# A two-layer DiT block on one core: fewer context columns in three projections, and scheduling priority for norm steps and evacuations

## The chip, the cores and the metric

The kernel runs on one core of a Trainium2 chip. A core has TensorE (matrix products, stationary operand loaded by a weight load, result in PSUM), VectorE, ScalarE and GpSimd, which run beside each other and wait for each other through semaphores, and DMA queues; all large loads here are issued by SyncE. The metric is the device time of one execution in microseconds, as a median over runs.

## The reference

Two layers work on 256 context rows and 256 latent rows of width 1024. Only the latent rows are returned, so in the last layer the context rows are needed for keys, values and recurrent states alone (`with_ctx` is false there).

```python
for l in range(DEPTH):                       # DEPTH = 2
    with_ctx = l < DEPTH - 1
    hx = rmsnorm(x, g_pre_mix[l]) * (1.0 + ax1) + sx1      # ax1, sx1, gx1 ...: c @ w_ada
    hc = rmsnorm(ctx, g_pre_mix[l]) * (1.0 + ac1) + sc1
    pc, px = split_cols(hc @ w_in + b_in), split_cols(hx @ w_in + b_in)
    # three mixers: mLSTM (q k v o i f), HGRN2 (q f i g), differential attention (q k v)
    yx = jnp.concatenate([mx, gx, ax], axis=-1) @ w_out    # and yc if with_ctx
    x = x + gx1 * rmsnorm(yx, g_post_mix[l])
    hx = rmsnorm(x, g_pre_ffn[l]) * (1.0 + ax2) + sx2
    x = x + gx2 * rmsnorm(swiglu(hx, ...), g_post_ffn[l])
    # the same for ctx if with_ctx
```

## The kernel before

**Rows and tiles.** The 512 rows are four tiles of 128: tiles 0 and 1 are context, 2 and 3 latent. `halves` is (1, 0) in the first layer (`full` is true there) and (1,) in the second: half 1 are tiles 2 and 3, half 0 tiles 0 and 1. `qt` is the list of tiles with queries: all four in the first layer, 2 and 3 in the second.

**Split products.** Each product is made of three matmuls on rounded f32 (fp32r). An operand is split into an upper part and the rest. Activations lie transposed in `hT[0]` and `hT[1]`. Weights come in blocks of 512 KB by SyncE (`wraw`, 3 buffers), ScalarE rounds them to `whi` (L297), VectorE subtracts to `wlo` (L298), with 2 buffers each and a priority of AHEAD = 2000. `mm` (L302) issues every one of these matmuls; the stationary operand is always 128 by 128.

**Projections.** `gemm_tm(srcs, act, tiles, evac, pre)` (L324) puts row tiles on the PSUM partitions: the activations are stationary and 256 weight columns move, for each of the tiles and 8 blocks of k. Two tiles share one PSUM bank, and an evacuation (`add_bias` L912, `ev_vo` L1062) takes a bank at a time. The differential attention's query, key columns (`O_DAQ`, 768 wide) go in three products of 256 columns, i = 0, 1, 2; so do the mLSTM's value and output gate (`O_MLV`) and query and key (`O_MLQ`). In each of these three groups the product i = 1 straddles the border at column 384 between two of the parts. `gemm_cm` (L368) keeps weights stationary and moves 256 or 512 activation columns; the feed-forward's gate and up projections use it.

**Between attention and feed-forward.** `head_norm` (L649) normalizes a head's output and writes it to Y; `rstd` (L412) does the power on GpSimd (L415, L416). `y_T` (L1147) transposes Y on TensorE and evacuates it with the gains into `hT` (ScalarE L1157, VectorE L1158). `out_first` and `out_rest` multiply with `w_out` (k blocks 4 to 7 first). `ev_z` (L1172) multiplies the result with the gate row on VectorE (L1175) and sums its squares on ScalarE (L1177). `post_norm` (L468) finishes that norm (VectorE L471, GpSimd L473) and adds the residual (VectorE L475). `norm_rows` (L424) squares R on ScalarE (L426), takes the power on GpSimd and scales on VectorE (L428). `norm_T` (L436) transposes that on TensorE (L447 ahead, L455) and evacuates it with scale and shift (ScalarE L461, VectorE L463), rounds to `hT[0]` (ScalarE L465) and subtracts to `hT[1]` (VectorE L466). `norm_T` also serves the next layer's first norm.

**Modulation.** The vectors for later stages are made from `w_ada` by VectorE sums (L226, L228: `acc`, `accq` from `araw`, 2 buffers) which the generator `ada_group` yields one by one; `ada_step` takes one after each weight block, and `ada_flush` the rest.

**Order.** The order on each engine is written out at compile time by a scheduler, which takes from the ready instructions of an engine the one of best priority; priority is the place in the program text, and `with tc.high_priority(offset=N)` moves instructions N places ahead. CHAIN is 4000. On the chip each engine then follows its written order and waits at its head. In the first layer the steps after attention have no such block; in the second one they have in part:

```python
if full:
    for t in (2 * hf, 2 * hf + 1):
        post_norm(t, Z[t], zss[t])
    norm_T(u1, s1_, hf, scr, ahead=False)
else:
    with tc.high_priority(offset=CHAIN):
        norm_T(u1, s1_, hf, scr)
```

Of the kernel before, what the change touches and what calls it, by code (L numbers as in the profile page):

```python
# [101 lines left out]
def dit_block(ctx: ExitStack, tc: tile.TileContext, x, c, ctx_in, c_ctx, w_ada, b_ada, g_pre_mix,  # L102
# [201 lines left out]
    def upper(ps, blk, act, t, first):  # L304
        hi, _, ks = blk
        for kk, k in enumerate(ks):
            mm(ps, act(0, k, t), hi[:, kk], first and kk == 0, False)
            mm(ps, act(1, k, t), hi[:, kk], False, False)

    def lower(ps, blk, act, t, last):  # L310
        _, lo, ks = blk
        for kk, k in enumerate(ks):
            mm(ps, act(0, k, t), lo[:, kk], False, last and k == ks[-1])

    def blocks_of(srcs, holds=None):

        k0 = 0
        for si, pieces in enumerate(srcs):
            nk, n = pieces[0].shape[0] // P, sum(p.shape[-1] for p in pieces)
            hi, lo = wload(pieces, holds and holds[si])  # L320
            yield hi[:, :, :n], lo[:, :, :n], range(k0, k0 + nk)
            k0 += nk

    def gemm_tm(srcs, act, tiles, evac, pre=None):  # L324

        n = sum(p.shape[-1] for p in srcs[0])
        tiles = list(tiles)
        wide = n > 256  # L330
        bank = lambda t: t if wide else t // 2
        banks = {b: pst([P, 512] if wide else [P, 2, 256], mm=True) for b in sorted({bank(t) for t in tiles})}
        dst = lambda t: banks[t][:, :n] if wide else banks[bank(t)][:, t % 2, :n]
        new = lambda t: wide or t - 1 not in tiles or t % 2 == 0
        for si, blk in enumerate(blocks_of(srcs)):
            end = si == len(srcs) - 1
            if pre is not None and end:
                pre()
            if wide and end:
                for t in tiles:  # L340
                    upper(dst(t), blk, act, t, si == 0)
                    lower(dst(t), blk, act, t, True)
                    evac([t], dst(t))
            else:

                for t in tiles:
                    upper(dst(t), blk, act, t, si == 0 and new(t))
                for t in tiles:
                    lower(dst(t), blk, act, t, end)
            ada_step()  # L350
        if not wide:
            for tb, b in banks.items():
                tt = [t for t in tiles if bank(t) == tb]
                evac(tt, b[:, tt[0] % 2:tt[-1] % 2 + 1, :n])
# [39 lines left out]
    def w_src(w, c0, n):  # L394
        return [[w[kh * 512:(kh + 1) * 512, c0:c0 + n]] for kh in range(2)]
# [40 lines left out]
    def norm_T(u, s, hf, scr, xs=None, ahead=True):  # L436
        r = 1 if hf == 0 else 0
        xn, hs = scr
        if xs is None:
            xs = [norm_rows(2 * hf + i, xn[:, i]) for i in range(2)]  # L440
        nah = NAH if ahead else 0
        pts = [pst([P, 2, 2, P]) for _ in range(nah)]

        for i in range(2):
            for kp in range(nah):
                for kk in range(2):
                    PE.transpose(pts[kp][:, kk, i, :], xs[i][:, (2 * kp + kk) * P:(2 * kp + kk + 1) * P], ident)  # L447
        for kp in range(KD // 2):
            if kp < nah:
                pt = pts[kp]  # L450
            else:
                pt = pst([P, 2, 2, P])
                for kk in range(2):
                    for i in range(2):
                        PE.transpose(pt[:, kk, i, :], xs[i][:, (2 * kp + kk) * P:(2 * kp + kk + 1) * P], ident)  # L455
            h = hs[:, kp % 2]
            for kk in range(2):
                k = 2 * kp + kk
                src = pt[:, kk].rearrange("p a b -> p (a b)")
# [149 lines left out]
    for l in range(DEPTH):  # L609
# [299 lines left out]
        hst.close()  # L909


        def add_bias(dst, w, nb, bb):  # L912
            return lambda tt, ps: V.tensor_tensor(dst[:, tt[0]:tt[-1] + 1, w:w + nb], ps[:, :, :nb],
                                                  bb.over(0, nb, len(tt)), op=ALU.add)

        qk = stg.tile([P, 4, 768], F32, tag="qk", name=nm("qk"))
        for i in range(3):
            bb = Bias([b_in[l, O_DAQ + i * 256:O_DAQ + (i + 1) * 256]])
            gemm_tm(w_src(w_in[l], O_DAQ + i * 256, 256), hact, qt if i == 0 else range(4), add_bias(qk, i * 256, 256, bb), pre=bb.load)
# [139 lines left out]
        for i in range(3):  # L1059
            bb = Bias([b_in[l, O_MLV + i * 256:O_MLV + (i + 1) * 256]])  # L1060

            def ev_vo(tt, ps, i=i, bb=bb):  # L1062
                c_ = 0
                while c_ < 256:
                    a = i * 256 + c_
                    if a < 384:
                        h, o = divmod(a, ML_D)
                        w = min(ML_D - o, 256 - c_, 384 - a)
                        V.tensor_tensor(Vml[:, tt[0]:tt[-1] + 1, h, o:o + w], ps[:, :, c_:c_ + w],
                                        bb.over(c_, c_ + w, len(tt)), op=ALU.add)  # L1070
# [8 lines left out]
            gemm_tm(w_src(w_in[l], O_MLV + i * 256, 256), hact, range(4) if i < 2 else qt, ev_vo, pre=bb.load)  # L1079
        mqk = stg.tile([P, 4, 768], F32, tag="qk", name=nm("mqk"))  # L1080
        for i in range(3):
            bb = Bias([b_in[l, O_MLQ + i * 256:O_MLQ + (i + 1) * 256]])
            gemm_tm(w_src(w_in[l], O_MLQ + i * 256, 256), hact, qt if i == 0 else range(4), add_bias(mqk, i * 256, 256, bb), pre=bb.load)

        dst_.close()
        gst = ExitStack()
# [60 lines left out]
        def y_T(hf, kps):  # L1147
            for kp in kps:
                pt = pst([P, 2, 2, P])
                for kk in range(2):  # L1150
                    for i in range(2):
                        PE.transpose(pt[:, kk, i, :], Y[2 * hf + i][:, (2 * kp + kk) * P:(2 * kp + kk + 1) * P], ident)
                for kk in range(2):
                    k = 2 * kp + kk
                    src = pt[:, kk].rearrange("p a b -> p (a b)")
                    dh = hT[0][:, k, hf * 256:hf * 256 + 256]
                    S.activation(dh, src, AF.Copy, scale=gcol[:, k:k + 1])  # L1157
                    V.scalar_tensor_tensor(out=hT[1][:, k, hf * 256:hf * 256 + 256], in0=src, scalar=gcol[:, k:k + 1],  # L1158
                                           in1=dh, op0=ALU.mult, op1=ALU.subtract)

        Z, zss = {}, {}

# [89 lines left out]
        with tc.tile_pool(name=f"ff{l}", bufs=1, reuse_waits="tile") as ff:  # L1252
# [122 lines left out]
```

## Time and profile before

| | |
|---|---|
| median of 3 runs | 1347.56 us (1346.56 to 1349.05) |
| the profiled execution | 1347.59 us, span 1345.9 us |
| TensorE busy | 1284.2 us, 95% of the span |
| VectorE, ScalarE, GpSimd busy | 898.6, 624.9, 202.3 us |
| mean granted TensorE clock | 0.985 of 2.4 GHz |

The span is from the first to the last instruction. Busy time is the union of an engine's instructions. PEld is TensorE's weight load, which overlaps its matmuls.

### The profile page before, as it was taken

To read this page: it belongs to the slowest core of one execution; us is meant where nothing else is said; L and a number is where in the kernel's file an instruction comes from. 1 tells how busy PE (TensorE), PEld (TensorE's weight loads), DVE (VectorE), ACT (ScalarE), POOL (GpSimd) and SP (SyncE) were. 2 spreads that over 40 slices of the span, in tenths; PEclk is the share of its full clock that TensorE was granted. 3 is DMA by queue.
4 is the path that set the end of the run, shared out by engine and by line. 5 is a ranking of instruction groups with operands and counts; after the bars stand their busy time and mean duration, and the time that the engine had idled before them with its cause. 6 is when DMAs were issued, how large, how long until landed. Compare 5 with 4: busy or idle time off the path is not lost.

```text
span 1345.9 us, 23128 instructions
## 1 busy us (share of the span) xinstructions
PE 1284.2 (95%) x9022; PEld 1094.6 (81%) x9022; DVE 898.6 (67%) x1564; ACT 624.9 (46%) x1188; POOL 202.3 (15%) x304
## 2 busy tenths in 40 slices
PE   7998999999989899999999999899999998999997
PEld 5785889778888798778887888778897998788886
DVE  4899998554688998476336348566855456666666
ACT  3436352578354653212221236546536724554543
POOL 3133202111142300001000003133111202000001
PEclk9999999999989999999999999899999999899999
DMA  9772526132244677477335235532331313456563
GB/s 290 227 221 75 164 64 201 41 114 72 95 141 142 192 253 229 141 255 243 116 100 178 94 111 151 148 95 63 104 95 51 122 47 109 142 188 188 188 188 125
DMA packets 158443, 194.05 MB, mean 144 GB/s; under 512 B 10524, under 2 KB 132806, under 8 KB 158334
## 3 DMA queue, kind: packets, MB, share of 16 engines
q1 hardware_dynamic: 156910, 188.89, 44.9%
q0 software_dynamic: 1424, 3.68, 1.0%
q8 instruction: 71, 1.16, 0.3%
q14 instruction: 38, 0.31, 0.1%
HBM read 191.47 MB, written 1.08 MB: 143 GB/s over the span
## 4 chain that ended last, share of the span: by engine, by line
PE 76%; DVE 10%; ACT 5%; issue 4%; DMA 3%; POOL 3%; SPq 0%; DVEq 0%; POOLq 0%; ACTq 0%
PE mm L302 62%; DMA araw<-in_w_ada_dram 2%; PE mx L1126 2%; DVE wlo L298 2%; PE mx L982 2%; PE mx L1003 1%; DVE acc L228 1%; PE mm L1114 1%; ACT whi L297 1%; POOL rstd L416 1%; PE mx L997 1%; PE mm L164 1%; DVE accq L228 1%; PE mx L880 1%; PE ada L233 1%
## 5 line engine op out<-in xcount | busy, mean ns | idle before, releaser
L297 ACT CAST whi<-wraw 128x1024 fp32r<-128x1024 f32 (+1 forms) x247 | 256.4, 1039 | 415.7 <-PE mm L302 365.2
L298 DVE TENSOR_TENSOR wlo<-wraw,whi 128x1024 fp32r<-128x1024 f32 (+1 forms) x243 | 295.8, 1218 | 193.0 <-PE mm L302 94.4
L302 PE MATMUL mm<-hT,whi 128*128 128x512 f32 (+1 forms) x1568 | 352.0, 372 | 4.4 <-ACT hT L465 2.1
L302 PEld LDWEIGHTS mm<-hT,whi 128*128 128x128 f32 x1568 | 270.8, 189 | 55.7 <-issue 4.0
L302 PE MATMUL mm<-whi,hT 128*128 128x256 f32 (+1 forms) x1792 | 264.3, 293 | 3.1 <-ACT hT L1157 1.4
L302 PEld LDWEIGHTS mm<-whi,hT 128*128 128x128 f32 x1792 | 234.0, 192 | 19.2 <-issue 8.4
L302 PE MATMUL mm<-hT,wlo 128*128 128x256 f32 (+1 forms) x960 | 185.0, 334 | 0.0
L302 PEld LDWEIGHTS mm<-hT,wlo 128*128 128x128 f32 x960 | 152.9, 190 | 21.1 <-issue 0.4
L302 PE MATMUL mm<-wlo,hT 128*128 128x256 f32 (+1 forms) x896 | 140.8, 292 | 0.0
L302 PE MATMUL mm<-whi,GT 128*128 128x512 f32 x504 | 129.5, 397 | 0.0
L302 PEld LDWEIGHTS mm<-wlo,hT 128*128 128x128 f32 x896 | 119.1, 191 | 10.9 <-issue 10.4
L302 PEld LDWEIGHTS mm<-whi,GT 128*128 128x128 f32 x504 | 93.7, 188 | 24.5 <-ACT whi L297 1.6
L228 DVE SCALAR_TENSOR_TENSOR accq<-araw,csil,accq 128x1024 f32<-128x1024 f32 x63 | 81.2, 1295 | 29.8 <-DMA araw<-in_w_ada_dram 29.7
L302 PE MATMUL mm<-wlo,GT 128*128 128x512 f32 x252 | 70.0, 396 | 0.0
L228 DVE SCALAR_TENSOR_TENSOR acc<-araw,csil,acc 128x1024 f32<-128x1024 f32 x49 | 62.8, 1306 | 4.6 <-DMA araw<-in_w_ada_dram 4.4
L302 PEld LDWEIGHTS mm<-wlo,GT 128*128 128x128 f32 x252 | 47.3, 188 | 11.3
L415 POOL TENSOR_SCALAR rstd<-hss 128x1 f32<-128x1 f32 (+2 forms) x44 | 18.8, 427 | 241.7 <-ACT hsq L656 159.9
L1327 POOL TENSOR_TENSOR Z<-Z,gg 128x512 f32<-128x512 f32 x6 | 9.4, 1572 | 234.1 <-ACT sqz L1326 234.1
L988 ACT ACTIVATE e<-mx,damx 128x512 f32<-128x512 f32 (+1 forms) x48 | 29.3, 618 | 26.3 <-DVE damx L985 26.3
L811 ACT COPY Ck<-Kh 128x512 f32<-128x512 f32 (+1 forms) x56 | 28.8, 525 | 25.7 <-DVE Kh L836 18.9
L416 POOL TENSOR_TENSOR rstd<-rstd,mhalf 128x1 f32<-128x1 f32 (+2 forms) x58 | 40.0, 690 | 4.7
L984 DVE TENSOR_REDUCE damx<-mx 128x1 f32<-128x512 f32 (+1 forms) x48 | 28.3, 598 | 18.0 <-PE mx L982 17.1
(283 smaller groups left out, 1499.9 us busy)
## 6 DMA issues: line engine op xcount, KB each, us to landing
araw<-in_w_ada_dram SPq DMA_DIRECT2D x80, 512.0 KB
wraw<-in_w_in_dram SPq DMA_DIRECT2D x68, 512.0 KB
wraw<-in_w_ffn_down_dram SPq DMA_DIRECT2D x50, 512.0 KB
wraw<-in_w_ffn_gate_dram SPq DMA_DIRECT2D x48, 512.0 KB
wraw<-in_w_ffn_up_dram SPq DMA_DIRECT2D x48, 512.0 KB
wraw<-in_w_out_dram SPq DMA_DIRECT2D x24, 512.0 KB
aw<-in_w_ada_dram SPq DMA_DIRECT2D x16, 512.0 KB
wraw<-in_w_in_dram SPq DMA_DIRECT2D x12, 256.0 KB
```

Of the source, the lines that this page charges most:

```text
L164: PE.matmul(acc0[3][:, :P], lhsT=ident, rhs=ident, start=True, stop=True, skip_group_check=True)
L228: V.scalar_tensor_tensor(out=a, in0=raw, scalar=csil[:, k, r:r + 1], in1=a, op0=ALU.mult, op1=ALU.add)
L297: S.copy(hi[:, :nk, :n], raw[:, :nk, :n])
L298: (eng or V).tensor_tensor(lo[:, :nk, :n], raw[:, :nk, :n], hi[:, :nk, :n], op=ALU.subtract)
L302: PE.matmul(ps, lhsT=lhs, rhs=rhs, start=first, stop=last, skip_group_check=True)
L415: G.tensor_scalar(o[:, :width], ss, 1.0 / n, EPS, ALU.mult, ALU.add)
L416: G.tensor_tensor(o[:, :width], o[:, :width], mhalf[:, :width], op=ALU.pow)
L811: S.copy(C[:, q0:].rearrange("p (a b i) -> p b a i", b=2, i=m), vap(K_, 2 * m * pq0, [[512 + m, 2], [2 * m, np_], [1, m]]))
L982: PE.matmul(pv[j], lhsT=qkT[0][64 * j:64 * j + DA_D, h, t * P:(t + 1) * P], rhs=qkT[1][64 * j:64 * j + DA_D, h, :nk], start=True, stop=True)
L984: V.reduce_max(mx[:, j:j + 1], pv[j], axis=AX.X)
L988: S.activation(e[:, j, :nk], pv[j], AF.Exp, bias=mx[:, 2 + j:3 + j], scale=sc, accum_out=mx[:, 4 + j:5 + j])
L1126: PE.matmul(po[:, i, d_, :], lhsT=W[d_, s_][0][:, t * P - W[d_, s_][2]:(t + 1) * P - W[d_, s_][2]], rhs=Vml[:, s_, h, :], start=n_ == 0, s ...
```

## The change

First, in the second layer three `gemm_tm` products, i = 1 of `O_DAQ`, `O_MLV` and `O_MLQ`, get `ctx_cols`: for tiles 0 and 1 their matmuls move only columns 128 to 256 (or 0 to 128 for `O_MLV`) of the 256, and `add_bias` evacuates those alone. The left out columns are queries and output gates of context rows, which nothing reads in that layer. Second, the evacuations of `norm_T` and `y_T` and all of `ev_z` are put under `high_priority(CHAIN)`, in both layers; and in the first layer `post_norm` and `norm_rows` of both halves are put under it too and called ahead of `norm_T`. The transposes and matmuls on TensorE stay outside the blocks.

```diff
-    def gemm_tm(srcs, act, tiles, evac, pre=None):
+    def gemm_tm(srcs, act, tiles, evac, pre=None, ctx_cols=None):
...
+        part = lambda t: slice(*ctx_cols) if ctx_cols and t < 2 else slice(0, n)
...
+            of = lambda t: (blk[0][:, :, part(t)], blk[1][:, :, part(t)], blk[2])
...
-                    upper(dst(t), blk, act, t, si == 0 and new(t))
+                    upper(dst(t)[:, part(t)], of(t), act, t, si == 0 and new(t))
                 for t in tiles:
-                    lower(dst(t), blk, act, t, end)
+                    lower(dst(t)[:, part(t)], of(t), act, t, end)
...
-            for kk in range(2):                       # norm_T
-                k = 2 * kp + kk
-                src = pt[:, kk].rearrange("p a b -> p (a b)")
-                if kk == 0:
-                    S.activation(h[:, kk], src, AF.Identity, bias=s(r, k), scale=u(r, k))
-                else:
-                    V.tensor_scalar(h[:, kk], src, u(r, k), s(r, k), ALU.mult, ALU.add)
-            sl = slice(hf * 256, hf * 256 + 256)
-            S.copy(hT[0][:, 2 * kp:2 * kp + 2, sl], h)
-            V.tensor_sub(hT[1][:, 2 * kp:2 * kp + 2, sl], h, hT[0][:, 2 * kp:2 * kp + 2, sl])
+            with tc.high_priority(offset=CHAIN):      # the same lines, in the block
...
+        need = lambda i, a, b: (a, b) if i == 1 and not full else None
+        def add_bias(dst, w, nb, bb, cc_=None):
+            def ev(tt, ps):
+                a, b = cc_ if cc_ and tt[0] < 2 else (0, nb)
+                V.tensor_tensor(dst[:, tt[0]:tt[-1] + 1, w + a:w + b], ps[:, :, a:b], bb.over(a, b, len(tt)), op=ALU.add)
+            return ev
...
-            gemm_tm(..., add_bias(qk, i * 256, 256, bb), pre=bb.load)
+            gemm_tm(..., add_bias(qk, i * 256, 256, bb, need(i, 128, 256)), pre=bb.load, ctx_cols=need(i, 128, 256))
...
-            gemm_tm(w_src(w_in[l], O_MLV + i * 256, 256), ..., ev_vo, pre=bb.load)
+            gemm_tm(w_src(w_in[l], O_MLV + i * 256, 256), ..., ev_vo, pre=bb.load, ctx_cols=need(i, 0, 128))
...
-                for kk in range(2):                   # y_T: L1157 and L1158
+                with tc.high_priority(offset=CHAIN):  # the same lines, in the block
...
-            V.tensor_mul(Z[t][:, cs_], ps, gg1[0 if t >= 2 else 1][:, cs_])   # ev_z
-            sq = sm.tile([P, 512], BF16, tag="sqz", name=nm("sqz"), bufs=1)
-            S.activation(sq, ps, AF.Square, accum_out=zss[t][:, j:j + 1])
+            with tc.high_priority(offset=CHAIN):      # the same lines, in the block
...
                 if full:
-                    for t in (2 * hf, 2 * hf + 1):
-                        post_norm(t, Z[t], zss[t])
-                    norm_T(u1, s1_, hf, scr, ahead=False)
+                    with tc.high_priority(offset=CHAIN):
+                        for t in (2 * hf, 2 * hf + 1):
+                            post_norm(t, Z[t], zss[t])
+                        xs = [norm_rows(t, scr[0][:, t - 2 * hf]) for t in (2 * hf, 2 * hf + 1)]
+                    norm_T(u1, s1_, hf, scr, xs, ahead=False)
```

## Rows read from the trace of the kernel before

**Rows 1.** The page, part 1: busy us, share of the span, instructions.

```profile
PE 1284.2 (95%) x9022; PEld 1094.6 (81%) x9022; DVE 898.6 (67%) x1564; ACT 624.9 (46%) x1188; POOL 202.3 (15%) x304
```

**Rows 2.** Busy time by stretch: length, PE, PEld, DVE, ACT, POOL, clock, DMA share, GB/s.

```profile
390.00:400.00 10.00, 6.26 (x36) 5.82 (x35) 9.14 (x14) 5.11 (x14) 5.22 (x6) 0.72 0.68 211
...
430.00:440.00 10.00, 8.32 (x37) 4.06 (x36) 7.37 (x11) 4.92 (x11) 5.55 (x8) 0.83 0.63 207
450.00:460.00 10.00, 6.85 (x57) 6.43 (x56) 10.00 (x18) 6.09 (x11) 2.20 (x3) 1.00 0.98 312
...
480.00:500.00 20.00, 20.00 (x170) 20.00 (x168) 19.66 (x22) 8.92 (x14) 0.00 (x0) 1.00 0.82 258
...
1062.00:1090.00 28.00, 28.00 (x236) 27.95 (x236) 10.14 (x13) 11.85 (x23) 5.05 (x10) 1.00 0.45 142
```

**Rows 3.** TensorE's groups in 390 to 480: busy us, mean ns, idle before, releasers.

```profile
L302 PE MATMUL mm<-whi,hT 128*128 128x256 f32 x194 | 30.3, 302 | 1.4 <-ACT hT L1157 1.4
L302 PE MATMUL mm<-hT,whi 128*128 128x256 f32 x112 | 15.7, 287 | 3.2 <-ACT hT L465 2.1 <-DVE hT L466 1.0
...
L1152 PE MATMUL mx<-ident,Y 128*128 128x128 f32 x24 | 5.0, 353 | 4.0 <-DVE Y L663 4.0
...
L455 PE MATMUL mx<-ident,nsc 128*128 128x128 f32 x32 | 4.7, 279 | 1.4 <-DVE nsc L428 1.4
```

**Rows 4.** Instructions in order of time: start us, us, engine, line, [idle before].

```profile
395.80 1.97 PE L1152 MATMUL mx<-ident,Y 128*128 128x128 f32 x8 [2.38 <-DVE Y L663]
...
426.99 0.15 DVE L471 TENSOR_SCALAR_CACHE_REDUCE zss<-zss 128x2 f32<-128x2 f32 x1
...
430.20 1.35 POOL L415 TENSOR_SCALAR rstd<-hss 128x2 f32<-128x2 f32 x1 [6.35 <-ACT hsq L656]
...
431.63 1.08 POOL L473 TENSOR_TENSOR rstd<-ss,mhalf 128x1 f32<-128x1 f32 x2
...
436.25 0.82 ACT L1157 ACTIVATE hT<-mx,gcol 128x256 fp32r<-128x256 f32 x2
...
452.45 1.21 DVE L298 TENSOR_TENSOR wlo<-wraw,whi 128x1024 fp32r<-128x1024 f32 x1
...
455.87 1.30 DVE L228 SCALAR_TENSOR_TENSOR acc<-araw,csil,acc 128x1024 f32<-128x1024 f32 x1
...
457.10 1.28 DVE L466 TENSOR_TENSOR hT<-nsc,hT 128x512 fp32r<-128x512 f32 x2
...
471.39 1.22 DVE L298 TENSOR_TENSOR wlo<-wraw,whi 128x1024 fp32r<-128x1024 f32 x1
...
473.36 1.03 PEld L302 LDWEIGHTS mm<-hT,wlo 128*128 128x128 f32 x8
...
1126.87 2.49 PE L302 MATMUL mm<-whi,hT 128*128 128x256 f32 x14 [0.33 <-DVE hT L1158]
```

**Rows 5.** VectorE's groups in 390 to 480: busy us, mean ns, idle before.

```profile
L298 DVE TENSOR_TENSOR wlo<-wraw,whi 128x1024 fp32r<-128x1024 f32 x20 | 24.5, 1225 | 1.1 <-ACT whi L297 0.9 <-issue 0.3
L228 DVE SCALAR_TENSOR_TENSOR accq<-araw,csil,accq 128x1024 f32<-128x1024 f32 x12 | 15.4, 1282 | 0.0
```

**Rows 6.** In order of time: runs of matmuls and weight loads back to back.

```profile
135.31 0.41 PEld L866 LDWEIGHTS mx<-Qd,Kh 128*128 128x128 f32 x2
...
416.99 1.99 PEld L302 LDWEIGHTS mm<-whi,hT 128*128 128x128 f32 x16
...
418.91 1.03 PEld L302 LDWEIGHTS mm<-wlo,hT 128*128 128x128 f32 x8
...
539.69 2.88 PE L302 MATMUL mm<-hT,whi 128*128 128x512 f32 x12
542.41 1.98 PE L302 MATMUL mm<-hT,wlo 128*128 128x512 f32 x8
...
1104.66 5.54 PEld L1126 LDWEIGHTS mx<-Vml,Dt 128*128 128x128 f32 x48
```

More of the change, by code (lines that the diff above doesn't have):

```diff
@@ L456, in norm_T @@
             h = hs[:, kp % 2]
-            for kk in range(2):
-                k = 2 * kp + kk
-                src = pt[:, kk].rearrange("p a b -> p (a b)")
-                if kk == 0:
-                    S.activation(h[:, kk], src, AF.Identity, bias=s(r, k), scale=u(r, k))
-                else:
-                    V.tensor_scalar(h[:, kk], src, u(r, k), s(r, k), ALU.mult, ALU.add)
-            sl = slice(hf * 256, hf * 256 + 256)
-            S.copy(hT[0][:, 2 * kp:2 * kp + 2, sl], h)
-            V.tensor_sub(hT[1][:, 2 * kp:2 * kp + 2, sl], h, hT[0][:, 2 * kp:2 * kp + 2, sl])
+            with tc.high_priority(offset=CHAIN):
+                for kk in range(2):
+                    k = 2 * kp + kk
+                    src = pt[:, kk].rearrange("p a b -> p (a b)")
+                    if kk == 0:
+                        S.activation(h[:, kk], src, AF.Identity, bias=s(r, k), scale=u(r, k))
+                    else:
+                        V.tensor_scalar(h[:, kk], src, u(r, k), s(r, k), ALU.mult, ALU.add)
+                sl = slice(hf * 256, hf * 256 + 256)
+                S.copy(hT[0][:, 2 * kp:2 * kp + 2, sl], h)
+                V.tensor_sub(hT[1][:, 2 * kp:2 * kp + 2, sl], h, hT[0][:, 2 * kp:2 * kp + 2, sl])
     def post_norm(t, Z, zss, out=None):
@@ L909, in dit_block @@
         hst.close()
-        def add_bias(dst, w, nb, bb):
-            return lambda tt, ps: V.tensor_tensor(dst[:, tt[0]:tt[-1] + 1, w:w + nb], ps[:, :, :nb],
-                                                  bb.over(0, nb, len(tt)), op=ALU.add)
+        need = lambda i, a, b: (a, b) if i == 1 and not full else None
[4 more added lines that the diff above has]
+            return ev
         qk = stg.tile([P, 4, 768], F32, tag="qk", name=nm("qk"))
@@ L918, in dit_block @@
             bb = Bias([b_in[l, O_DAQ + i * 256:O_DAQ + (i + 1) * 256]])
-            gemm_tm(w_src(w_in[l], O_DAQ + i * 256, 256), hact, qt if i == 0 else range(4), add_bias(qk, i * 256, 256, bb), pre=bb.load)
+            gemm_tm(w_src(w_in[l], O_DAQ + i * 256, 256), hact, qt if i == 0 else range(4), add_bias(qk, i * 256, 256, bb, need(i, 128, 256)),
+                    pre=bb.load, ctx_cols=need(i, 128, 256))
         bb = Bias([b_in[l, O_DAV:O_DAV + 256]])
@@ L1078, in ev_vo @@
                     c_ += w
-            gemm_tm(w_src(w_in[l], O_MLV + i * 256, 256), hact, range(4) if i < 2 else qt, ev_vo, pre=bb.load)
+            gemm_tm(w_src(w_in[l], O_MLV + i * 256, 256), hact, range(4) if i < 2 else qt, ev_vo, pre=bb.load, ctx_cols=need(i, 0, 128))
         mqk = stg.tile([P, 4, 768], F32, tag="qk", name=nm("mqk"))
@@ L1082, in dit_block @@
             bb = Bias([b_in[l, O_MLQ + i * 256:O_MLQ + (i + 1) * 256]])
-            gemm_tm(w_src(w_in[l], O_MLQ + i * 256, 256), hact, qt if i == 0 else range(4), add_bias(mqk, i * 256, 256, bb), pre=bb.load)
+            gemm_tm(w_src(w_in[l], O_MLQ + i * 256, 256), hact, qt if i == 0 else range(4), add_bias(mqk, i * 256, 256, bb, need(i, 128, 256)),
+                    pre=bb.load, ctx_cols=need(i, 128, 256))
         dst_.close()
@@ L1152, in y_T @@
                         PE.transpose(pt[:, kk, i, :], Y[2 * hf + i][:, (2 * kp + kk) * P:(2 * kp + kk + 1) * P], ident)
-                for kk in range(2):
[L1154 to L1159, printed above, removed]
+                with tc.high_priority(offset=CHAIN):
+                    for kk in range(2):
+                        k = 2 * kp + kk
+                        src = pt[:, kk].rearrange("p a b -> p (a b)")
+                        dh = hT[0][:, k, hf * 256:hf * 256 + 256]
+                        S.activation(dh, src, AF.Copy, scale=gcol[:, k:k + 1])
+                        V.scalar_tensor_tensor(out=hT[1][:, k, hf * 256:hf * 256 + 256], in0=src, scalar=gcol[:, k:k + 1],
+                                               in1=dh, op0=ALU.mult, op1=ALU.subtract)
         Z, zss = {}, {}
@@ L1174, in ev_z @@
             cs_ = slice(j * 512, (j + 1) * 512)
-            V.tensor_mul(Z[t][:, cs_], ps, gg1[0 if t >= 2 else 1][:, cs_])
-            sq = sm.tile([P, 512], BF16, tag="sqz", name=nm("sqz"), bufs=1)
-            S.activation(sq, ps, AF.Square, accum_out=zss[t][:, j:j + 1])
+            with tc.high_priority(offset=CHAIN):
+                V.tensor_mul(Z[t][:, cs_], ps, gg1[0 if t >= 2 else 1][:, cs_])
+                sq = sm.tile([P, 512], BF16, tag="sqz", name=nm("sqz"), bufs=1)
+                S.activation(sq, ps, AF.Square, accum_out=zss[t][:, j:j + 1])
         def out_first(hf):
```

## Prediction

> **What bounds the kernel now.** I read the page first: TensorE is busy for 1284.2 of the 1345.9 us of the span [rows 1]. So the whole kernel is a TensorE queue with a few holes, and the question for each edit is whether it closes a hole or shortens the queue. The second view is the busy time by stretch, which finds the holes near the edits [rows 2]. In the first layer, between attention and feed-forward, TensorE is busy 6.26 us of 390 to 400, 8.32 us of 430 to 440 and 6.85 us of 450 to 460. From 480 on it is full. The granted clock is 0.72 in the first of these stretches and 0.83 in the second: a part of each ran at 1.2 GHz instead of 2.4 GHz, after TensorE had stood idle. In the second layer, where the narrowed products stand, TensorE is full as well: 28.00 of 28 us in 1062 to 1090 [rows 2]. The third view is the groups of TensorE's own instructions in 390 to 480, with what ended the idle time before them [rows 3]. It adds up to 10.0 us: 4.0 us waiting for Y from VectorE, 1.4 us for the ScalarE part of y_T's evacuation (hT L1157), 3.2 us for norm_T's two evacuations (2.1 hT L465, 1.0 hT L466), and 1.4 us for the scaled rows of the norm (nsc L428). That is all there is to win from the priorities, together with the clock. The fourth view, the order in time, shows what was ahead of the late instruction on its engine [rows 4].
>
> **Part 1: narrowed products.** In the second layer the context tiles 0 and 1 need only half of the 256 columns in three products (DA i=1, ML value i=1, ML query/key i=1). That is 3 products x 2 tiles x 8 k x 3 terms = 144 matmuls that go from 256 to 128 moving columns. No matmul, weight load or DMA is dropped. Two bias additions work on half the columns; VectorE is 36% busy there (10.14 of 28 us), so they are worth nothing.
>
> What is one narrow matmul worth? Today a split-weight matmul of 256 columns starts every (418.91 - 416.99) / 16 = 0.120 us, and one of 512 columns every (542.41 - 539.69) / 12 = 0.227 us [rows 6]. The slope is 0.107 us per 256 columns, so 128 columns fewer would save 0.053 us and give 0.067 us, if only columns counted. But each of these matmuls has a new stationary tile of 128 columns. The nearest row with the same stationary size and few moving columns is the plain f32 product of 97 columns: 48 weight loads in 5.54 us, one of them 0.19 us long, so (5.54 - 0.19) / 47 = 0.114 us apiece [rows 6]. A plain f32 matmul of 256 columns costs 0.41 - 0.19 = 0.22 us [rows 6], 0.86 ns a column, so 97 columns alone would be 0.083 us; the missing 0.03 us is the weight load that can't be hidden behind so short a stream. I take 0.114 us: a gain of 0.006 us x 144 = 0.9 us, say 1.0. The bounds are 0.067 us (gain 144 x 0.053 = 7.6 us) and, should the narrow form lose its rate and cost as much as the 256-column plain f32 row, 0.22 us (loss 144 x 0.10 = 14 us). A split-weight matmul of 128 columns does not occur before, so both ends stay in the range.
>
> The row says that a short stream does not get below 0.114 us. The Trainium skill (TensorE: Matmul & The Clock Gate, LDWEIGHTS) has a weight load last in proportion to its columns, P / 1.2 ns, which is 107 ns for 128 columns, and says that f32 gains nothing from the fast weight load; by that the three products gain about 1.9 us. The same page's isolated gap of N / 2.4 + 2.5 ns would give 56 ns and a gain of 9 us. The measured 0.114 us is on the side of the first.
>
> **Part 2: priorities.** No instruction is added. Evacuations and norm steps are moved ahead of the weight splits (whi on ScalarE, wlo on VectorE, themselves 2000 places ahead) and of the modulation sums (accq), which fill VectorE: 20 splits take 24.5 us and 12 accq sums 15.4 us of these 90 us [rows 5]. A step moved in front of one split gains at most about 1.2 us, and only if it was ready when the split started.
>
> *y_T at 390 to 402.* ScalarE's half of the evacuation costs TensorE 1.4 us here [rows 3], in part because a split and a head norm's square are ahead of it. But TensorE's next work are transposes of Y, which wait 2.38 of the 4.0 us (at 395.80, [rows 4]) for a head norm that is not moved. Earlier evacuations let a few more matmuls in and free the PSUM tiles: I take 0.7 us (bounds 0 and 2).
>
> *Post-norm at 427 to 441.* The last sum of squares (zss) is done at 427.1, yet the power that uses it (L473 on GpSimd) runs at 431.63, in a queue behind a head norm's step that waited 6.35 us for ScalarE. The two L473 (1.08 us) in turn stand ahead of that head norm's own power, on which Y and so the rest of TensorE's wait for Y (4.0 - 2.4 = 1.6 us) depend [rows 3, 4]. If L473 goes ahead, Y is 1.1 us earlier, and the residual and its squares are off ScalarE when y_T's evacuation, now at 436.25, is ready; I put that at another 0.9. Together 2.0 us (bounds 0 and 3.5).
>
> *norm_T at 452 to 458.* The split at 452.45 (1.21 us) goes before the gate product and the shift of the norm; then a modulation sum at 455.87 (1.30 us) runs while the last subtraction becomes ready, which starts at 457.10 [rows 4]. The first is removed by priority (1.2 us); the second only where the step is ready in the scheduler's own order, so I count half, 0.6 us. Together 1.8 of the 3.2 us (bounds 0 and 3.2). The 1.4 us before L455 I leave, since the context half's norm has the other half's first feed-forward products beside it (4 x 48 matmuls of 0.120 us, 23 us).
>
> *What it gives back.* The same priority holds for the context half, which is not urgent. A split at 471.39 ends at 472.61 and its matmuls start at 473.36 [rows 4], a slack of 0.75 us; a subtraction pair (1.28 us, as at 457.10) ahead of it makes TensorE wait 0.5 us. Two such pairs cost 1.0 us; five such steps (both subtraction pairs, both residuals, the scaled rows) at the same 0.53 us would cost 2.6 us, the upper bound; 0 below. The modulation sums and the SP loads behind them come later too; they are hidden by the feed-forward, where TensorE stays full, and cost nothing unless the last group misses the next layer's start.
>
> *Second layer.* y_T, the first gate product and norm_T carry the priority there too; TensorE's wait for y_T is 0.33 us [rows 4], and the rest was in a priority block already. Nothing.
>
> **Sum.** 0.7 + 2.0 + 1.8 + 1.0 - 1.0 = 4.5 us less. The profiled execution took 1347.59 us (span 1345.9), 0.03 above the median of the runs. Prediction: 1347.6 - 4.5 = 1343.1 us. Likely case's own range: 1339.5 to 1344.9.
>
> **Rivals.**
> - *More than that.* TensorE's clock doesn't fall at 394 and 435 any more. In 390 to 400 a clock of 0.72 means 5.6 us at the lower level; half of the work in it, about 2 us, comes back, and 1 us of the other. With most of the 10 us of idle time gone and the narrow matmuls at 0.067 us (the gap rule above), that is 7 + 3 + 7.6 - 1 = 16 us: 1331. Half of it is more plausible: 1336. For it: the idle time is really there. Against: 2.4 us of Y's wait is not touched.
> - *No change.* TensorE's program order stays, so it goes on waiting at the same heads for Y, and the narrow matmuls are bound by their weights: gain 1 to 2 us, less the give-back. About 1347. For it: 4.0 of the 10.0 us hang on a head norm outside the blocks.
> - *Slower through starved splits.* VectorE is 98% busy in 480 to 500 and full in 450 to 460 [rows 2]. If the order written by the scheduler puts norm steps ahead of splits before their inputs have come on the chip, VectorE stands at its head and each block of 24 matmuls (2.9 us) waits. It decides from about two stalls of a whole split (1.2 us) more than I counted; with six it costs 7 us, less 2 gained: about 1352. For it: the slack of 0.75 us. Against: sums worth 1.28 us each are still there as filler to be pushed back first.
> - *Slower through the narrow form.* At 0.22 us it costs 14 us, less 3.5: about 1358. It decides from 0.145 us on, where 144 x 0.025 equals the 3.5 us of the priorities. Against: its stream is half as long as one that takes 0.120 us.
>
> **Chances.** Forecast 0.45, more than that 0.15, no change 0.18, starved splits 0.14, narrow form 0.08. The measurement tells 0.2% (2.7 us) from no change. Faster: 0.45 + 0.15, and a little of the no-change case, 0.61; same 0.18; slower 0.21. Eight in ten: from 1335.5, leaving out the far half of the large gain, to 1352, leaving out the slow narrow form and the worst of the starving.
>
> **What the profile after would show.** Right: matmuls of 128 columns on the three products' tile at about 0.114 us apiece; L473 before 430; TensorE's idle time before hT L465 and L466 in 450 to 460 at 1 to 2 us; TensorE full from 480 on. Wrong: a weight load period of 0.07 or 0.2 us there; new TensorE waits for whi or wlo in 440 to 480; a wait on accq or araw near the second layer's start.

## The result, and the profile after

The changed kernel takes 1365.36 us in the median (1362.09 to 1367.78), against 1347.06 us for the kernel before in the same session. The ratio is 1.0133, interval 1.0105 to 1.016: the change costs 18 us. The forecast of 1343.1 us and its range to 1352 us are both missed, on the slow side.

The profiled execution took 1367.12 us, with a span of 1365.4 us and a mean granted clock of 0.975 (before 0.985). Line numbers moved: the evacuations of y_T are now L1168 and L1169, those of norm_T L466 to L469, the power of post_norm L476, its residual L478, the head norm's power L418 and its product L666.

Part 1 of the page after, against [rows 1]:

```profile
PE 1298.1 (95%) x9022; PEld 1105.6 (81%) x9022; DVE 899.6 (66%) x1564; ACT 622.2 (46%) x1186; POOL 203.8 (15%) x304
```

TensorE issues the same 9022 matmuls, 144 of them half as wide, and is busy 13.9 us longer. Its share is 95% as before, so the share tells nothing here. The Trainium skill (Perfetto Trace Analysis, Identifying the Most-Contended Engine) says of a matmul's busy share that it does not measure the distance to the limit; these two rows agree.

Busy time by stretch after, the columns as in [rows 2]:

```profile
390.00:400.00 10.00, 7.44 (x44) 5.60 (x42) 9.74 (x20) 5.11 (x14) 4.83 (x6) 1.00 0.64 205
430.00:440.00 10.00, 5.95 (x21) 2.44 (x20) 8.96 (x12) 4.22 (x12) 4.67 (x6) 0.88 0.40 121
440.00:450.00 10.00, 8.48 (x46) 8.08 (x47) 7.41 (x10) 2.76 (x4) 6.01 (x12) 0.61 0.55 184
450.00:460.00 10.00, 8.28 (x67) 7.60 (x66) 9.95 (x15) 7.27 (x16) 2.02 (x2) 1.00 0.80 258
...
855.80:1108.80 253.00, 243.28 (x1969) 211.25 (x1968) 145.64 (x310) 124.83 (x267) 45.95 (x76) 0.94 0.29 85
```

The first layer's four stretches show what was hoped for at 390 to 400 and 450 to 460 (7.44 for 6.26 us, 8.28 for 6.85 us) and a new hole at 430 to 450; the kernel before has 8.32 us in 430 to 440 [rows 2], and in 440 to 450:

```profile
440.00:450.00 10.00, 9.69 (x81) 9.44 (x80) 10.00 (x13) 5.51 (x9) 4.38 (x9) 1.00 0.37 116
```

The last row after is the second layer from the norm's last transposes to those of the mLSTM's query and key. The same work in the kernel before, in the same view:

```profile
853.20:1089.00 235.80, 230.69 (x1969) 200.22 (x1968) 145.79 (x310) 127.21 (x269) 47.46 (x76) 1.00 0.31 92
```

Same number of TensorE's instructions, 17.2 us more. Of these 4.6 us are idle time (9.7 for 5.1 us) and 12.6 us are busy time, and the clock is 0.94 for 1.00. So nearly the whole loss lies in the layer that I costed at a gain of 1.0 us.

**Where in the second layer.** Start of the first or last matmul of a stage, us from the start of the span:

| | before | after | difference |
|---|---|---|---|
| norm of the first layer's end, first transposes of its feed-forward (layer 0) | 439.90 | 442.82 | +2.9 |
| second layer, norm's last transposes | 853.22 | 855.83 | +2.6 |
| HGRN mixer, last product | 974.61 | 980.68 | +6.1 |
| attention, padded transposes | 998.89 | 1008.61 | +9.7 |
| attention, last score product | 1049.45 | 1064.19 | +14.7 |
| mLSTM, transposes of query and key | 1089.07 | 1108.84 | +19.8 |
| end | 1345.87 | 1365.42 | +19.6 |

While a mixer waits for VectorE and ScalarE, TensorE fills the gap with a projection that is needed later. Before, one of them is the second block of DAQ, in the HGRN mixer, three gaps in a row (TensorE in order of time: start, us, line, [idle before and its releaser]):

```profile
953.53 1.92 PE L302 MATMUL mm<-whi,hT 128*128 128x256 f32 x14
955.42 0.33 PE L823 MATMUL mx<-Qd,Ck 128*32 128x32 f32 x16
955.68 1.34 PE L302 MATMUL mm<-whi,hT 128*128 128x256 f32 x9
956.95 0.33 PE L823 MATMUL mx<-Qd,Ck 128*32 128x32 f32 x16
957.21 1.22 PE L302 MATMUL mm<-whi,hT 128*128 128x256 f32 x8
958.26 0.28 PE L302 MATMUL mm<-wlo,hT 128*128 128x256 f32 x1
```

The same three gaps after:

```profile
955.92 1.00 PE L302 MATMUL mm<-whi,hT 128*128 128x128 f32 x7
957.80 0.33 PE L826 MATMUL mx<-Qd,Ck 128*32 128x32 f32 x16 [0.88 <-DVE Qd L842]
958.06 0.77 PE L302 MATMUL mm<-whi,hT 128*128 128x128 f32 x5
959.13 0.33 PE L826 MATMUL mx<-Qd,Ck 128*32 128x32 f32 x16 [0.30 <-DVE T L846]
959.39 1.34 PE L302 MATMUL mm<-whi,hT 128*128 128x128 f32 x6
```

Where 14, 9 and 9 wide matmuls stood, TensorE's program now has 7, 5 and 6 (the last are three narrow and three wide). They run out early, TensorE waits, and the granted clock falls to half at 959.8 us. The stretches with the fallen clock in the second layer, up to the transposes of query and key (busy time by stretch, the clock is the third number from the end):

```profile
959.80:963.20 3.40, 3.40 (x41) 2.89 (x44) 2.91 (x11) 2.19 (x7) 0.00 (x0) 0.50 0.11 39
970.00:976.80 6.80, 6.80 (x32) 6.22 (x30) 5.23 (x19) 1.26 (x4) 0.00 (x0) 0.50 0.27 77
1034.80:1041.70 6.90, 6.90 (x32) 6.53 (x32) 3.73 (x12) 2.69 (x7) 0.00 (x0) 0.51 0.34 97
1048.50:1055.30 6.80, 6.80 (x31) 6.04 (x29) 3.12 (x7) 4.29 (x10) 0.59 (x2) 0.50 0.00 0
1062.20:1069.00 6.80, 6.80 (x25) 5.18 (x25) 2.69 (x6) 2.47 (x7) 0.00 (x0) 0.50 0.01 2
```

Together these are 30.7 us at 1.2 GHz. The kernel before has no such stretch here; both only end an earlier one at the start (2.0 us before, 1.6 us after). Fully busy at half speed, the 30.7 us cost up to 15.4 us against the 12.6 us of added busy time. The Trainium skill (TensorE: Matmul & The Clock Gate, HAM oscillation — how this bites in real kernels) describes a kernel whose short bursts between waits run cold again and again, and advises a loop order that keeps TensorE fed; the trace agrees, with these five falls, and none where the gaps were filled. The waits of that kernel are for DMA and longer than those here, which are for VectorE and ScalarE and last 1.43 us at most.

**In the first layer.** TensorE's groups in 390 to 480 after, against [rows 3]:

```profile
L302 PE MATMUL mm<-whi,hT 128*128 128x256 f32 x192 | 31.8, 308 | 5.7 <-DVE hT L1169 2.9 <-ACT hT L1168 2.5
L302 PE MATMUL mm<-hT,whi 128*128 128x256 f32 x96 | 13.5, 289 | 1.5 <-ACT hT L468 1.0 <-DVE hT L469 0.2 <-ACT whi L297 0.2
...
L1162 PE MATMUL mx<-ident,Y 128*128 128x128 f32 x24 | 3.7, 289 | 1.9 <-DVE Y L666 1.9
```

The wait in norm_T's row fell from 3.2 to 1.5 us (0.2 us of it now for a split) and that for Y from 4.0 to 1.9 us; the wait in the first row, for y_T's evacuations, rose from 1.4 to 5.7 us. The last half of Y in order of time, after, against the rows from 430.20 to 436.25 of [rows 4]:

```profile
433.40 0.19 POOL L417 TENSOR_SCALAR rstd<-hss 128x2 f32<-128x2 f32 x1 [6.25 <-ACT hsq L659]
433.68 1.08 POOL L476 TENSOR_TENSOR rstd<-ss,mhalf 128x1 f32<-128x1 f32 x2
434.26 2.48 DVE L478 SCALAR_TENSOR_TENSOR R<-Z,rstd,R 128x1024 f32<-128x1024 f32 x2 [0.69 <-POOL rstd L476]
434.71 1.40 POOL L418 TENSOR_TENSOR rstd<-rstd,mhalf 128x2 f32<-128x2 f32 x1
...
436.66 0.54 DVE L666 SCALAR_TENSOR_TENSOR Y<-Oml,rstd,Y 128x96 f32<-128x96 f32 x2
437.03 0.94 PE L1162 MATMUL mx<-ident,Y 128*128 128x128 f32 x4 [1.90 <-DVE Y L666]
...
438.01 0.47 ACT L1168 ACTIVATE hT<-mx,gcol 128x256 fp32r<-128x256 f32 x1 [1.27 <-PE mx L1162]
...
438.49 2.18 DVE L228 SCALAR_TENSOR_TENSOR acc<-araw,csil,acc 128x1024 f32<-128x1024 f32 x1
...
440.60 0.47 DVE L1169 SCALAR_TENSOR_TENSOR hT<-mx,gcol,hT 128x256 fp32r<-128x256 f32 x1
...
441.12 1.30 PE L302 MATMUL mm<-whi,hT 128*128 128x256 f32 x4 [1.79 <-DVE hT L1169]
```

Post_norm's power L476 did not pass the head norm: it still stands behind L417, which waits 6.25 us for ScalarE, and ahead of the head norm's L418. What the priority did move are both residuals (L478, 2.48 us): they now run on VectorE ahead of Y's product L666. Y comes late, but the residuals hold it up by only about 0.6 us (L418 ends at 436.11, L666 starts at 436.66): the head norm's step L417 itself starts at 433.40 us for the 430.20 us of L415 before, and these rows don't show why. Then a modulation sum (L228, 2.18 us) stands ahead of L1169, and TensorE waits another 1.79 us. The clock of 440 to 450 is 0.61.

### The profile page after: what moved, and what is told of

It reads as the page before. It is cut to its first block, busy times and chain, and to the rows that moved or that the text cites. A ratio compares the mean times of both kernels' runs of the same rounds, so it can differ in the third digit from the quotient of the medians.

```text
span 1365.4 us, 23116 instructions
## 1 busy us (share of the span) xinstructions
PE 1298.1 (95%) x9022; PEld 1105.6 (81%) x9022; DVE 899.6 (66%) x1564; ACT 622.2 (46%) x1186; POOL 203.8 (15%) x304
## 4 chain that ended last, share of the span: by engine, by line
PE 77%; DVE 9%; ACT 5%; issue 4%; POOL 3%; DMA 1%; SPq 0%; POOLq 0%; DVEq 0%; ACTq 0%
PE mm L302 63%; PE mx L1136 2%; PE mx L991 2%; DVE wlo L298 2%; PE mx L1012 1%; POOL rstd L418 1%; PE mx L1006 1%; PE mm L1124 1%; ACT whi L297 1%; PE mx L883 1%; PE ada L233 1%; PE mm L164 1%; DVE Qd L842 1%; POOL rstd L417 1%; PE mx L858 1%
## 5 line engine op out<-in xcount | busy, mean ns | idle before, releaser
L302 PE MATMUL mm<-whi,hT 128*128 128x256 f32 (+2 forms) x1792 | 273.0, 299 | 7.3 <-DVE hT L1169 3.3
L302 PEld LDWEIGHTS mm<-whi,hT 128*128 128x128 f32 x1792 | 240.8, 198 | 28.0 <-issue 12.0
L302 PE MATMUL mm<-wlo,hT 128*128 128x256 f32 (+2 forms) x896 | 141.8, 295 | 0.0
L228 DVE SCALAR_TENSOR_TENSOR accq<-araw,csil,accq 128x1024 f32<-128x1024 f32 x63 | 81.1, 1296 | 27.8 <-DMA araw<-in_w_ada_dram 27.7
L228 DVE SCALAR_TENSOR_TENSOR acc<-araw,csil,acc 128x1024 f32<-128x1024 f32 x49 | 64.5, 1341 | 4.7 <-DMA araw<-in_w_ada_dram 4.5
L417 POOL TENSOR_SCALAR rstd<-hss 128x1 f32<-128x1 f32 (+2 forms) x44 | 17.9, 406 | 256.2 <-ACT hsq L659 171.7
L418 POOL TENSOR_TENSOR rstd<-rstd,mhalf 128x1 f32<-128x1 f32 (+2 forms) x58 | 42.7, 737 | 4.6
L991 PE MATMUL mx<-qkT,qkT 48*128 48x512 f32 (+1 forms) x96 | 36.7, 580 | 4.2 <-ACT e L997 3.6
```

The source lines that it names most:

```text
L228: V.scalar_tensor_tensor(out=a, in0=raw, scalar=csil[:, k, r:r + 1], in1=a, op0=ALU.mult, op1=ALU.add)
L302: PE.matmul(ps, lhsT=lhs, rhs=rhs, start=first, stop=last, skip_group_check=True)
L417: G.tensor_scalar(o[:, :width], ss, 1.0 / n, EPS, ALU.mult, ALU.add)
L418: G.tensor_tensor(o[:, :width], o[:, :width], mhalf[:, :width], op=ALU.pow)
L991: PE.matmul(pv[j], lhsT=qkT[0][64 * j:64 * j + DA_D, h, t * P:(t + 1) * P], rhs=qkT[1][64 * j:64 * j + DA_D, h, :nk], start=True, stop=True)
```

## The experiments

The theory after this reading has two parts. **A:** the narrow products lose because TensorE's program puts fewer of them into each gap of a mixer, not because a narrow matmul is slow; and the priorities lose through post_norm's block alone. **Rivals:** the narrow form itself is slow; or the prioritised evacuations starve the splits of weights. The ratios are to the kernel before, on the same chip.

### The priorities alone

```diff
-        need = lambda i, a, b: (a, b) if i == 1 and not full else None
+        need = lambda i, a, b: None
```

> The priorities as in the change, all products with full width. Where the trace after stands against the one before, about 3 us are lost by the end of the first layer and 16 to 17 us in the second. If the priorities own the first loss alone: 1349 to 1351 us, TensorE waiting for Y at about 437 as in the trace after, second layer as before. Rival, that the priorities own the loss in the second layer too (norm_T and y_T carry them there): 1360 us or more.

Measured 1351.58 us, ratio 1.0033 (1.002 to 1.0045). So the priorities lose 4.4 us, slightly more than expected, and do not gain the 3.5 us of the forecast. One row, here of the kernel before and of this one, TensorE's busy time in 390 to 480, serves from here on:

```profile
390.00:480.00 90.00, 80.06 (x593) 73.58 (x592) 80.12 (x141) 52.32 (x109) 24.92 (x36) 0.94 0.55 176
...
390.00:480.00 90.00, 78.64 (x555) 70.98 (x554) 78.98 (x136) 48.74 (x105) 28.41 (x38) 0.92 0.55 170
```

In these 90 us TensorE starts 555 matmuls; the kernel before starts 593. At 0.120 us for each of the 38 that come later [rows 6] that is 4.6 us, about the loss. The changed kernel, with the same priorities, starts 566 (3.2 us); the five kernels below that have no priority start 591 to 596, which is the scatter of the count.

### The narrow products alone

All four priority blocks are taken out (those of y_T, norm_T and ev_z serve both layers), the three narrow products stay.

```diff
-            with tc.high_priority(offset=CHAIN):
+            if True:
```

> The three narrowed products alone, no priorities. If they own the loss of the second layer: 1347 + 16 = 1363 us (1360 to 1366), the clock falling between 950 and 1070 as in the trace after. Rival, that the loss comes from the priorities: 1344 to 1347 us.

Measured 1365.69 us, ratio 1.0133 (1.0103 to 1.0163; the runs scatter from 1358.0 to 1369.4). The whole loss is there without any priority. The two halves together, 18.5 and 4.4 us, are more than the 18.3 us of the change, but the scatter of this run is larger than the difference.

### One narrow product where TensorE has no gaps

Only the second block of MLQ is narrow, which stands between other projections after the attention.

> Only the mLSTM query/key product i = 1 is narrow (48 matmuls of 128 columns); no priorities. TensorE's order is that of before, matmul for matmul. Theory of the order (the loss comes from fewer matmuls being written into the gaps of the mixers, where the other two products stand): 48 x 0.011 to 0.013 us less, 1346.5 us, within 0.2% of before. Theory of the width (a 128 column matmul costs the chip more, or lets the clock fall wherever it runs): a third of 16 us more, 1352 us, with the granted clock below 1 beside this product.

Measured 1345.96 us, ratio 0.9991 (0.9982 to 1.0001): no loss, and no gain that can be told. Its trace has the 9022 matmuls in the very order of the kernel before, and so on VectorE, ScalarE and GpSimd; with all three narrow the order departs from it at the first narrow filling of the HGRN mixer. It is also the place to read the price of a narrow matmul (weight loads in order of time; the first two rows are half narrow, half wide, the others wide):

```profile
1070.33 3.78 PEld L302 LDWEIGHTS mm<-whi,hT 128*128 128x128 f32 x32
...
1074.04 1.93 PEld L302 LDWEIGHTS mm<-wlo,hT 128*128 128x128 f32 x16
...
1075.89 3.91 PEld L302 LDWEIGHTS mm<-whi,hT 128*128 128x128 f32 x32
...
1081.65 3.91 PEld L302 LDWEIGHTS mm<-whi,hT 128*128 128x128 f32 x32
```

The mixed 48 take 5.56 us, the wide 48 take 5.76 us. The 24 narrow ones save 0.20 us, 0.008 us each: a narrow matmul takes 0.112 us. The narrow form is not slow.

### Almost full width

The context tiles take 240 of 256 columns in the three products in place of 128; no priorities.

```diff
-    ... need(i, 128, 256) ...   need(i, 0, 128)
+    ... need(i, 16, 256) ...    need(i, 0, 240)
```

> As the three narrowed products alone, but with 240 of the 256 columns for the context tiles in place of 128; no priorities. The order written for TensorE has as few matmuls, or fewer, in each gap of the mixers as with 128. Theory of the order: as slow as with 128 columns or slower, 1360 to 1370 us, the clock falling in 950 to 1070, though TensorE moves 94% of the columns. Theory of the width: as before, 1346 to 1348 us.

Measured 1366.72 us, ratio 1.0145 (1.0131 to 1.0158). Sixteen columns fewer cost as much as 128 fewer. In the three gaps shown above, TensorE of this kernel:

```profile
953.12 0.71 PE L302 MATMUL mm<-whi,hT 128*128 128x240 f32 x4
954.99 0.33 PE L826 MATMUL mx<-Qd,Ck 128*32 128x32 f32 x16 [1.16 <-DVE Qd L842]
955.26 0.49 PE L302 MATMUL mm<-whi,hT 128*128 128x240 f32 x2
956.33 0.33 PE L826 MATMUL mx<-Qd,Ck 128*32 128x32 f32 x16 [0.58 <-DVE T L846]
956.59 1.00 PE L302 MATMUL mm<-whi,hT 128*128 128x240 f32 x3
```

4, 2 and 3 matmuls where 14, 9 and 9 stood, though they last no longer than the wide ones. The filling does not follow the length on the chip. It is TensorE's program that has fewer of them: 32 wide, 9 of 240 columns, 15 of 128 (18 with the three wide ones). That would fit an order written as if each column of a narrowed matmul counted about four times (240 x 4 / 256 = 3.75, 128 x 4 / 256 = 2); the counts suggest it, and no run tests it.

### The two filling products apart

One kernel narrows the second block of DAQ alone, the other that of MLV alone; no priorities.

> No priorities; of the three narrowed products only the second block of DAQ is narrow, which TensorE uses to fill the gaps of the HGRN mixer. Theory (each narrowed product that fills a mixer's gaps costs its own share: 3.1 us in the mixer and 3.7 us of matmuls that come later, as the milestones of the changed kernel put it): 1353 to 1355 us. Rival (the loss belongs to the attention's gaps, or to the clock that the two stretches share): within 2 us of before.

> No priorities; of the three narrowed products only the second block of MLV is narrow, which TensorE uses to fill the gaps of the attention. Theory (own share: 5.0 us in the attention and 5.0 us of matmuls that come later, by the milestones of the changed kernel): 1355 to 1358 us. Rival (the attention's loss only follows from the mixer's before it): within 2 us of before.

Measured 1354.54 us (ratio 1.0058, 1.0045 to 1.0072) and 1357.47 us (1.0078, 1.0058 to 1.0098): 8.0 and 10.9 us, together 18.9 us for the 18.5 us of all three. Each pays its own share in its own mixer. Busy time by stretch with DAQ narrow, then with MLV narrow:

```profile
960.00:970.00 10.00, 10.00 (x81) 8.89 (x82) 6.70 (x17) 5.70 (x20) 0.00 (x0) 0.50 0.08 16
...
1050.00:1060.00 10.00, 9.94 (x59) 7.14 (x58) 5.47 (x14) 7.10 (x20) 2.00 (x6) 1.00 0.01 2
```

```profile
960.00:970.00 10.00, 9.74 (x108) 8.74 (x108) 8.91 (x28) 6.46 (x23) 0.00 (x0) 1.00 0.18 54
...
1050.00:1060.00 10.00, 10.00 (x25) 5.25 (x25) 4.45 (x11) 3.25 (x11) 1.24 (x4) 0.50 0.01 2
```

The low clock is in the mixer whose filling was narrowed and not in the other. These two traces also tell what the loss is made of. From the same matmul ahead of the first narrowed gap (953.29 us before) to the transposes of query and key (1089.07 us), the same 1102 matmuls in each kernel:

| kernel | us | TensorE idle, us | at 1.2 GHz, us |
|---|---|---|---|
| before | 135.8 | 2.1 | 0 |
| DAQ narrow | 143.9 | 3.1 | 17.1 |
| MLV narrow | 149.8 | 3.2 | 30.7 |
| all three narrow | 151.4 | 5.3 | 30.7 |
| 240 columns | 155.9 | 6.2 | 37.6 |

Of the 8.1 and 14.0 us that one product alone loses here (the profiled execution with MLV narrow is the slowest of its runs), about 1 us each is idle time. The rest goes with the lower clock, which at half speed can cost up to 8.5 and 15.4 us. Nor did TensorE stand idle ahead of each fall: with MLV narrow the clock is at half from 1024.4 us, and TensorE had been busy for 10.20 of the 10.40 us before.

### Which priority loses

All at full width: without the priority on post_norm's block, with y_T's alone, with norm_T's alone, and with all four and the head norm's chain of the first layer put under the same priority. The blocks of y_T and norm_T serve the second layer too.

```diff
+            with tc.high_priority(offset=CHAIN if full else 0):
                 rd = sm.tile([P, 2, 2], F32, tag="rd", name=nm("rd"), bufs=4)
...
                 head_norm(Oml, (2 * hf, 2 * hf + 1), ML_D, h * ML_D, None, True)
```

> Full width everywhere; priority on the evacuations of y_T, ev_z and norm_T, but the block of post_norm and norm_rows of layer 0 left without. Theory A (the loss of 4.4 us of the priorities alone comes from post_norm overtaking the head norm, which the transposes of Y wait for): the gap of 1.9 us ahead of those transposes is gone, the gains at the y_T and norm_T evacuations of about 2 us each stay, and the time is 1343 to 1346 us. Rival B (the loss comes from the evacuations of y_T or norm_T themselves, which push the splits of weights back): 1350 to 1353 us, as with all four.

> Full width; priority on the evacuations of y_T alone. Theory A (post_norm overtaking the head norm is the loss): about 2 us faster than before where the first transposes of Y of layer 0 stand, 1345 to 1347 us in all. Rival B (the prioritised evacuations of Y are themselves the loss, since they pass the head norm's steps on VectorE and ScalarE): 1349 to 1352 us, with a gap ahead of the later transposes of Y.

> Full width; priority on the evacuations of norm_T alone. Theory A: the two gaps among the norm's transposes shrink from 2.1 and 1.0 us to about 0.5 and 1.0 us, nothing else moves, and the time is 1345 to 1347 us. Rival B (the steps passed over are splits that the weights of the gate wait for): the gain comes back as waits for weights, 1347 to 1350 us.

> Full width; all the priorities of the change, and the head norm's chain of the matrix memory's halves of layer 0 (from rd on to head_norm) under the same priority, so that post_norm no longer passes it. Theory A (passing the head norm is the loss): the gap of 1.9 us ahead of the last transposes of Y of half 0 and the low clock after it go, and the time is 1342 to 1346 us, 6 to 9 us below the kernel with the priorities alone (1351.6). Rival B (the loss is the splits and accumulations that everything prioritised passes): 1349 to 1354 us.

And y_T's and norm_T's priority together, and norm_T's with the narrow MLQ:

> Full width; priority on the evacuations of y_T and of norm_T, without that on ev_z and on the block of post_norm. If the two gains add (1.6 and 3.1 us): 1342 to 1343 us. If each only takes away the same fall of the clock near 395 us or the same wait: 1344 to 1346 us, like the kernel that has ev_z's priority too.

> The two parts that gained or cost nothing alone, together: priority on the evacuations of norm_T, and the narrow second block of MLQ. If the two add (0.9 and 3.1 us): 1342.5 to 1344 us. If the narrow block's share was only the scatter of the runs: 1344 to 1345 us. Slower than 1346 us would show that one undoes the other.

| first layer's priorities | us | ratio (interval) | matmuls started in 390 to 480 |
|---|---|---|---|
| none (before) | 1347.2 | | 593 |
| all four | 1351.58 | 1.0033 (1.002 to 1.0045) | 555 |
| without post_norm's block | 1344.98 | 0.9982 (0.9973 to 0.9991) | 610 |
| y_T alone | 1345.62 | 0.9987 (0.9978 to 0.9996) | 605 |
| norm_T alone | 1344.11 | 0.9977 (0.9968 to 0.9986) | 617 |
| y_T and norm_T | 1344.69 | 0.9987 (0.9978 to 0.9997) | 605 |
| all four and the head norm | 1345.40 | 0.9992 (0.9983 to 1.0001) | 617 |
| norm_T, and MLQ narrow | 1343.33 | 0.9971 (0.9962 to 0.9981) | 617 |

The times come from three sessions, each with its own runs of the kernel before (1347.15 us for all four, 1346.56 us for y_T with norm_T and for the last row, 1347.19 us for the others); the ratios are what can be compared.

Without post_norm's block the loss of 4.4 us is a gain of 2.2. I had expected the gap ahead of Y's transposes to go with it. It did not: TensorE's groups in 390 to 480 of that kernel still hold 2.3 us for Y.

```profile
L302 PE MATMUL mm<-whi,hT 128*128 128x256 f32 x196 | 30.1, 296 | 3.1 <-ACT hT L1168 2.2 <-DVE hT L1169 0.9
...
L1162 PE MATMUL mx<-ident,Y 128*128 128x128 f32 x24 | 5.2, 369 | 2.3 <-DVE Y L666 2.3
```

What went is the wait for L1169: 2.9 us in the changed kernel, 0.9 us here. With the head norm ahead as well, Y's wait goes, 1.9 to 0, and with it the loss, yet this is no faster than the others. The wait for the same evacuation (there L1170) is 3.1 us again, and TensorE waits 2.5 us for splits, which the head norm has presumably pushed back:

```profile
L302 PE MATMUL mm<-whi,hT 128*128 128x256 f32 x199 | 30.5, 299 | 3.6 <-DVE hT L1170 3.1 <-ACT hT L1169 0.4
...
L302 PE MATMUL mm<-wlo,hT 128*128 128x256 f32 x104 | 15.3, 289 | 2.5 <-DVE wlo L298 2.5
```

So the loss is the block's, but which of its steps makes it is not shown: one kernel is rid of it by a shorter wait for L1169, the other by a shorter wait for Y.

The gains of y_T and norm_T did not add. With both, the wait for norm_T is 2.5 us, as with y_T alone, where norm_T alone has it at 1.1 us (with both, then norm_T alone):

```profile
L302 PE MATMUL mm<-hT,whi 128*128 128x256 f32 x125 | 18.2, 295 | 2.5 <-ACT hT L468 1.5 <-DVE hT L469 1.1
...
L302 PE MATMUL mm<-hT,whi 128*128 128x256 f32 x128 | 17.6, 287 | 1.1 <-ACT hT L468 0.6 <-DVE hT L469 0.5
```

The traces show why: with both, every instruction on TensorE, VectorE, ScalarE and GpSimd stands in the same place as with y_T alone. Beside y_T's block norm_T's priority changed nothing in the order written, so this kernel is the one of y_T alone measured again (ratio 0.9987 both times), and no test of two gains together. norm_T alone came out 0.9 us below the range expected for it.

The last kernel of the table is the lowest of all, 0.3% below before; from norm_T's priority alone it can't be told. It is the version to keep, or norm_T's priority by itself.

## Why the prediction was wrong

- **Part 1, the step from "No matmul, weight load or DMA is dropped" to a cost of the matmuls' own time alone, failed.** The price was right: 0.112 us measured for 0.114 taken, worth 0.008 us x 144 = 1.2 us for 1.0. It was taken from plain f32 rows, and there a product of the program stands as two matmuls of the trace (L866: 16 products, 32 matmuls), so that the rows' 0.114 and 0.22 us are each one of the two. That the 0.114 us fits a split-weight matmul is in part luck, and the reason that I gave, a weight load that can't be hidden, is not shown. But I looked at the second layer in one stretch, 1062 to 1090, where TensorE is full [rows 2]. Two of the three products stand in the gaps of the mixers, and there their worth is not their length: it is the gap that they fill and the clock that they hold. A new width in these places wrote a new order for TensorE, and that order filled the three gaps shown half as well. Measured 18.5 us of loss, most of it at the lower clock: 8.0 for DAQ, 10.9 for MLV, none for MLQ. The almost full width shows that what the chip saves by the width has no part in it.
- **The rival of the narrow form** (1358 us) gave a loss, 10 us for 18, for the wrong reason; its price of 0.22 us is refuted by 0.112 us. No rival of mine had the order of TensorE change with the width.
- **Part 2, the post-norm step, had the wrong sign.** "If L473 goes ahead, Y is 1.1 us earlier": it did not go ahead. It waits in GpSimd's queue behind the head norm's step, which has no priority, as I had noted. Only the residuals passed Y on VectorE, and held it up by about 0.6 us. I had counted 2.0 us of gain with a lower bound of 0; all priorities measured 4.4 us of loss, and 2.2 us of gain without this block. I had given this step no bound on the side of a loss, though the head norm that it shares GpSimd with stood in the same rows.
- **norm_T** was right in place, and in size as a wait: 3.2 to 1.5 us in the changed kernel (1.8 taken). In time that edit alone gave 3.1 us, near the upper bound of 3.2, with 24 more matmuls in 390 to 480 (24 x 0.120 = 2.9 us).
- **y_T** gained 1.6 us alone for 0.7 taken, inside its bounds of 0 and 2. That the gains of y_T and norm_T add, as the sum has it, is not borne out: the two alone (0.9987 and 0.9977) would make 0.9964, and both together measured 0.9978 to 0.9997, since norm_T's priority moved no instruction where y_T had one.
- **Starved splits** did not decide: in 390 to 480 the changed kernel waits 0.2 us for a split. They came only when the head norm was moved too, 2.5 us. That this rival's 1352 us is what the priorities alone took is chance. The second layer's other priorities changed nothing, as forecast: from the transposes of query and key to the end it takes 256.6 us for 256.8.
- **What stays open.** How the loss in the second layer divides is read from traces, not set by an edit: in the changed kernel the idle time (4.6 us) and at most half of the 30.7 us at the lower clock (15.4 us), less the narrow matmuls' 1.2 us, make 18.8 us for 17.2 measured. Narrow DAQ and MLV products in the order of the kernel before were not tried; only MLQ kept that order. Why the order written is another one, and which step of post_norm's block loses, is not known.

## What to carry to other kernels

A matmul that fills another stage's gap is worth the gap and the clock that it holds, not its own length. Before making such work shorter, see where it stands in TensorE's order, and afterwards count how many stand in each gap: a cheaper instruction can have the whole order written anew. Priority given to one link of a chain can be lost, or worse, if the link stands in a queue behind a step without it. Here the loss went when the head norm had it too (ratio 0.9992), and there was none when norm_T's evacuations alone had it (0.9977). Test such edits singly, and compare the orders in the traces: one of them left every instruction where it was.

## What the runs showed of the hardware

A split-weight matmul of 240 columns with a new stationary tile starts as often as one of 128 columns: in the kernel with 240 columns the same mixed 48 matmuls take 5.54 us (weight loads from 1086.07 to 1091.61 us), with 128 columns 5.56 us, and 48 of 256 columns 5.76 us. So 16 columns fewer than 256 already give all that half the width gives, and the 0.112 us lie close to the 0.114 us of the 97-column f32 row [rows 6].

With MLV narrow the clock stood at half for 30.7 us of the attention, though in the 149.8 us around it TensorE was idle for only about 1 us more than before: what changed is what TensorE did in the gaps, not how long it waited.
